# Rotary embedding: unit 0's second half loaded by one SyncE transfer with 16 KB rows and stored from GpSimd

## The chip, the cores and the metric

One core of a Trainium2 chip. The metric is the device time of one execution in microseconds (us). In the profile PE is TensorE, DVE VectorE, ACT ScalarE, POOL GpSimd, SP SyncE. L72 is line 72 of the kernel, and the lines of the changed kernel and of the experiments are shifted by a few. A ratio below is the mean time of one kernel's fast runs over that of the other's of the same rounds, so not quite the ratio of the medians quoted beside it. Each experiment was timed beside the kernel before on the same chip.

## The reference

```
angles = outer(positions * scale, freqs)          # 1024 x 32
cos, sin = cos(angles), sin(angles)
out_first  = x_first * cos - x_second * sin       # x: 8 x 8 x 1024 x 64, float32
out_second = x_first * sin + x_second * cos
```

16.8 MB are read and 16.8 MB written; the arithmetic is small. The sin/cos table is made on the core, from two tiny inputs: positions (8 KB) and frequencies (128 bytes).

## The kernel before

x is cut into four units of 4 MB, each spread over 128 partitions with 8192 values a row. GpSimd's loads cast float32 to float16 on the way. Only the second half of unit 0 is loaded as float32 (X0f) and cast by ScalarE, which brings it in without GpSimd.

```
X0f = xout.tile([P, N], FP32, tag="O")
Q = NH // 2                                                         # NH = 4096 values, 16 KB
nc.sync.dma_start(out=X0f[:, :Q], in_=xv[0][:, NH : NH + Q])        # 1 MB, 8 KB rows
nc.scalar.dma_start(out=pos_i64, in_=positions...)                  # 128 rows of 64 B
nc.scalar.dma_start(out=freq_row, in_=freqs[None, :])               # 1 row of 128 B
nc.scalar.dma_start(out=X0f[:, Q:NH], in_=xv[0][:, NH + Q :])       # 1 MB, 8 KB rows
...
nc.gpsimd.dma_start(out=Xf[0][:, :NH], in_=xv[0][:, :NH])           # unit 0, first half, cast
for u in range(1, NU): nc.gpsimd.dma_start(out=Xf[u], in_=xv[u])    # units 1 to 3, cast
... # table: matmul of freq_row, VectorE, two sines, 16 matmuls that spread it, copies to T
nc.scalar.copy(out=Xf[0][:, NH:], in_=X0f[:, :NH])                  # behind the copies to T
for u in range(NU):
    for s in range(2):                                              # halves
        ... # VectorE: two products, one subtraction, one addition
        nc.scalar.copy(out=OUT[:, ns], in_=Xf[u][:, ns])
        if u in (0, NU - 1):
            nc.sync.dma_start(out=ov[u][:, ns], in_=OUT[:, ns])     # 2 MB
    if u not in (0, NU - 1):
        nc.gpsimd.dma_start(out=ov[u], in_=OUT)                     # 4 MB
```

The order on each engine is pinned to the order of the program.

## Time and profile before

84.41 us, median of 6 runs (84.1 to 84.78); the profiled execution has a span of 82.5 us.

| what | us |
|---|---|
| positions land / frequencies land | 5.74 / 5.45 |
| the table's first step on VectorE (y) starts | 6.22 |
| first product of the main loop starts | 13.07 |
| unit 2's store is issued | 59.37 |
| VectorE's last instruction ends | 69.5 |

To read it, look for what can be late without cost. VectorE is busy without a gap in the main loop, but it ends 13 us before the span does; the DMA engines are at work almost from end to end. The lines are in the prediction.

### The profile page before, as it was taken

What the parts mean: (1) busy time and instruction counts of PE and PEld (TensorE: products, weight loads), DVE (VectorE), ACT (ScalarE), POOL (GpSimd) and SP (SyncE); (2) the same over time, 40 slices, a digit from 0 to 9 for tenths busy, and PEclk for the clock granted to TensorE, in tenths of its full rate; (3) what the DMA queues carried; (4) which work ended last, traced back from release to release, by engine and by line L of the source; (5) the groups of instructions that cost most, each with busy time, mean ns of one, the idle gap of its engine ahead of it and who ended that gap; (6) DMA issues with size and microseconds to landing.
All of it is one profiled execution on the core that took longest, in us unless ns stands there. A gap on an engine that the chain in (4) does not pass through costs nothing.

```text
span 82.5 us, 179 instructions
## 1 busy us (share of the span) xinstructions
PE 7.1 (9%) x18; PEld 2.8 (3%) x18; DVE 60.3 (73%) x40; ACT 40.1 (49%) x18; POOL 4.6 (6%) x14
## 2 busy tenths in 40 slices
PE   0020999200000000000000000000000000000000
PEld 0020333000000000000000000000000000000000
DVE  0306476999999999999999999999999997000000
ACT  0603069999950790393098059219606902940000
POOL 4920000000000000000000200000200000000000
PEclk9999999985555555555555555555555555555555
DMA  2899998997996999799979999996998999799990
GB/s 48 336 319 278 290 326 187 254 246 159 230 254 127 254 262 342 270 278 350 278 191 302 270 342 421 461 524 286 508 509 350 413 508 461 302 445 429 397 485 24
DMA packets 1874, 26.22 MB, mean 318 GB/s; under 512 B 338, under 2 KB 338, under 8 KB 338
## 3 DMA queue, kind: packets, MB, share of 16 engines
q0 software_dynamic: 864, 15.73, 66.2%
q1 hardware_dynamic: 720, 9.44, 27.5%
q10 hardware_dynamic: 290, 1.06, 3.3%
HBM read 16.79 MB, written 16.78 MB: 407 GB/s over the span
## 4 chain that ended last, share of the span: by engine, by line
DVE 55%; ACT 15%; issue 6%; DMA 5%; PE 5%; DVEq 1%; ACTq 0%
DVE X L153 20%; DVE pr L152 20%; DVE X L157 9%; DVE X L154 6%; DMA freq_row<-in_freqs_dram 5%; ACT T L139 5%; ACT OUT L160 4%; PE ps L129 4%; ACT X L140 4%; DVEq L193 1%; PE cfreq L97 1%; ACT tab L122 1%; DVE r L113 1%; DVE y L104 1%; ACTq L69 0%
## 5 line engine op out<-in xcount | busy, mean ns | idle before, releaser
L160 ACT CAST OUT<-X 128x4096 f32<-128x4096 f16 x8 | 28.9, 3607 | 24.2 <-DVE X L157 24.2
L152 DVE TENSOR_TENSOR pr<-X,T 128x4096 f16<-128x4096 f16 x8 | 18.3, 2292 | 1.0 <-ACT T L139 0.7
L153 DVE TENSOR_TENSOR X<-X,T 128x4096 f16<-128x4096 f16 x8 | 18.3, 2292 | 0.3
L154 DVE TENSOR_TENSOR X<-X,pr 128x2048 f16<-128x2048 f16 x8 | 9.8, 1225 | 0.3
L157 DVE TENSOR_TENSOR X<-pr,X 128x2048 f16<-128x2048 f16 x8 | 9.7, 1218 | 0.0
L139 ACT CAST T<-ps 128x1024 f16<-128x1024 f32 x6 | 5.7, 1028 | 2.6 <-PE ps L129 2.6
L129 PE MATMUL ps<-tab,sel 128*128 128x512 f16 x16 | 6.5, 599 | 2.2 <-ACT tab L122 2.2
L164 POOL DMA_DIRECT2D out_dram<-OUT x2 | 1.1, 538 | 54.1 <-ACT OUT L160 54.1
L137 DVE CAST T<-ps 128x1024 f16<-128x1024 f32 x2 | 2.5, 1225 | 2.2 <-PE ps L129 2.2
L140 ACT CAST X<-X0f 128x4096 f16<-128x4096 f32 x1 | 3.6, 3649 | 0.0
L95 DVE COPY sel<-one 128x2048 f16<-128x2048 f16 x1 | 0.7, 693 | 2.8 <-POOL one L87 2.8
L129 PEld LDWEIGHTS <-sel 128*128 128x128 f16 x16 | 2.3, 143 | 6.1 <-issue 6.1
L117 ACT ACTIVATE tab<-r 128x256 f16<-128x256 f32 x1 | 0.4, 418 | 4.1 <-DVE r L113 4.1
L117 ACT ACT_TABLE_LOAD x1 | 1.3, 1283 | 2.1 <-issue 2.1
L92 POOL DMA_DIRECT2D X<-in_x_dram x3 | 2.0, 658 | 0.0
L100 DVE CAST posf<-pos_i 128x8 f32<-128x8 int32 x1 | 0.2, 172 | 2.3 <-DMA pos_i<-in_positions_dram 2.3
L97 PE MATMUL cfreq<-freq_row,coef 1*128 1x32 f32 x2 | 0.6, 392 | 5.6 <-DMA freq_row<-in_freqs_dram 5.6
L83 POOL DMA_DIRECT2D X<-in_x_dram x1 | 0.7, 669 | 0.8 <-POOLq L179 0.8
L97 PEld LDWEIGHTS cfreq<-freq_row,coef 1*128 1x128 f32 x2 | 0.5, 306 | 5.6 <-issue 5.6
L104 DVE TENSOR_TENSOR y<-posf,cfreq 128x256 f32<-128x256 f32 x1 | 0.4, 422 | 0.3 <-PE cfreq L97 0.3
L122 ACT ACTIVATE tab<-ra,quarter 128x256 f16<-128x256 f32 x1 | 0.5, 507 | 0.0
L113 DVE SCALAR_TENSOR_TENSOR r<-m,y 128x256 f32<-128x256 f32 x1 | 0.4, 424 | 0.0
(10 smaller groups left out, 1.9 us busy)
## 6 DMA issues: line engine op xcount, KB each, us to landing
out_dram<-OUT SPq DMA_DIRECT2D x4, 2048.0 KB, 14.8
out_dram<-OUT POOLq DMA_DIRECT2D x2, 4096.0 KB, 15.3
X<-in_x_dram POOLq DMA_DIRECT2D x3, 2048.0 KB, 31.9
X0f<-in_x_dram SPq DMA_DIRECT2D x1, 1024.0 KB, 4.8
X<-in_x_dram POOLq DMA_DIRECT2D x1, 1024.0 KB, 11.7
X0f<-in_x_dram ACTq DMA_DIRECT2D x1, 1024.0 KB, 13.2
pos_i<-in_positions_dram ACTq DMA_DIRECT2D x1, 8.0 KB, 5.0
freq_row<-in_freqs_dram ACTq DMA_DIRECT2D x1, 0.1 KB
```

Of the source, the lines that this page charges most:

```text
L92: pin(nc.gpsimd.dma_start(out=Xf[u], in_=xv[u]))
L97: nc.tensor.matmul(out=cfreq, lhsT=coef, rhs=freq_row, start=True, stop=True)
L117: pin(nc.scalar.activation(out=tab[:, 0], in_=r, func=AF.Sin, bias=0.0, scale=-_TWO_PI_DN))
L129: nc.tensor.matmul(out=ps[:, i].rearrange("p t w -> p (t w)"), lhsT=sel[:, g + i].rearrange("s h q -> s (h q)"), rhs=tab.rearrange("s t k ...
L137: pin(nc.vector.tensor_copy(out=dst, in_=ps))
L139: pin(nc.scalar.copy(out=dst, in_=ps))
L140: pin(nc.scalar.copy(out=Xf[0][:, NH:], in_=X0f[:, :NH]))
L152: pin(nc.vector.tensor_tensor(out=pr, in0=Xs, in1=sin_b, op=ALU.mult))
L153: pin(nc.vector.tensor_tensor(out=Xs, in0=Xs, in1=cos_b, op=ALU.mult))
L154: pin(nc.vector.tensor_tensor(out=Xs[:, :, 0, :], in0=Xs[:, :, 0, :], in1=pr[:, :, 1, :], op=ALU.subtract))
L157: pin(nc.vector.tensor_tensor(out=Xs[:, :, 1, :], in0=pr[:, :, 0, :], in1=Xs[:, :, 1, :], op=ALU.add))
L160: pin(nc.scalar.copy(out=OUT[:, ns], in_=Xf[u][:, ns]))
```

## The change

The intent: one transfer with larger rows instead of two for X0f, ScalarE's queue free for the small inputs, and the store of unit 0's second half behind GpSimd's loads, so that it takes no DMA time from them.

```
-    Q = NH // 2
-    pin(nc.sync.dma_start(out=X0f[:, :Q], in_=xv[0][:, NH : NH + Q]))
+    pin(nc.sync.dma_start(out=X0f[:, :NH], in_=xv[0][:, NH:]))
...
-    pin(nc.scalar.dma_start(out=X0f[:, Q:NH], in_=xv[0][:, NH + Q :]))
...
             if u in (0, NU - 1):
-                pin(nc.sync.dma_start(out=ov[u][:, ns], in_=OUT[:, ns]))
+                eng = nc.gpsimd if (u, s) == (0, 1) else nc.sync
+                pin(eng.dma_start(out=ov[u][:, ns], in_=OUT[:, ns]))
```

## The prediction

> **What bounds the kernel now.** I read the page first: the share of each engine, the row of DMA over 40 slices, the three DMA queues. VectorE is busy 73% of the span; the 16 DMA engines are busy nearly always.
>
> ```profile
> DVE  0306476999999999999999999999999997000000
> ACT  0603069999950790393098059219606902940000
> DMA  2899998997996999799979999996998999799990
> ...
> q0 software_dynamic: 864, 15.73, 66.2%
> q1 hardware_dynamic: 720, 9.44, 27.5%
> q10 hardware_dynamic: 290, 1.06, 3.3%
> HBM read 16.79 MB, written 16.78 MB: 407 GB/s over the span
> ```
>
> The reader is to see two candidates for the bound: VectorE without a gap from slice 7 to 33, and DMA at 8 or 9 almost from end to end (q0 is GpSimd's queue, q1 SyncE's, q10 ScalarE's; the three add up to 97% of 16 engines' span). Packets are counted where they start, so single slices wobble; the table by stretches of 10 us settles it (the last two figures of a row are the DMA share and GB/s):
>
> ```profile
> 2.00:12.00 10.00, 4.18 (x11) 1.91 (x12) 4.35 (x8) 3.20 (x4) 2.60 (x7) 1.00 1.00 301
> ...
> 42.00:52.00 10.00, 0.00 (x0) 0.00 (x0) 9.86 (x6) 6.56 (x2) 0.54 (x1) 0.50 1.08 356
> 52.00:62.00 10.00, 0.00 (x0) 0.00 (x0) 9.86 (x7) 3.63 (x2) 0.53 (x1) 0.50 1.00 429
> 62.00:72.00 10.00, 0.00 (x0) 0.00 (x0) 7.42 (x5) 6.05 (x2) 0.00 (x0) 0.50 0.96 416
> 72.00:81.00 9.00, 0.00 (x0) 0.00 (x0) 0.00 (x0) 1.17 (x1) 0.00 (x0) 0.50 0.96 411
> ```
>
> From 2 to 81 us the DMA engines have no idle stretch. So the kernel is bound by DMA: 79 us of packets, a start of about 1.8 us before the first byte and about 1.3 us after the last. A reordering of the same bytes can't shorten 79 us; it can only open a hole. The question is then whether the DMA engines are ever left without work, and that is set by when stores become ready, that is by the chain of computation. The chain of waits over the first 17 us (start, duration, what):
>
> ```profile
> 1.16 4.29 DMA freq_row<-in_freqs_dram
> 5.45 0.14 issue
> 5.58 0.61 PE cfreq L97 x2
> 6.20 0.02 issue
> 6.22 0.43 DVE y L104
> ...
> 8.42 3.59 PE ps L129 x8
> ```
>
> and of VectorE's list of waits:
>
> ```profile
> DVE posf L100 <- DMA pos_i<-in_positions_dram: 2.3, 1, 2.3
> ...
> DVE pr L152 <- ACT T L139: 0.7, 1, 0.7
> ```
>
> So the main loop starts when the sin/cos table T is spread, at 13.07 us, and the table starts when two tiny transfers on ScalarE's queue land: frequencies at 5.45, positions at 0.74 + 5.0 = 5.74. From 13.07 on VectorE runs to 69.5 without waiting for anything. A delay of the tiny transfers goes one to one into every store.
>
> **What the Trainium skill says.** "DMA: Bandwidth & Descriptors", section "Queues, rings and completion order": each DMA engine goes round-robin over the queue rows that have work, a packet a turn. The trace agrees, and tells the size of a turn. This is the DMA view of the 0.64 us from 3.50 (packets, MB, share of 16 engines):
>
> ```profile
> q1 hardware_dynamic: 34, 0.28, 102.6%
> q10 hardware_dynamic: 33, 0.00, 3.5%
> ```
>
> 34 rows of 8 KB against 33 rows of 64 B: one for one. Turns go by rows, not by bytes. A row of 8 KB takes 1.026 x 16 x 0.64 / 34 = 0.309 us, a 64 B row about 0.011 us. The same page, section "Issuing engines are not separate DMA queues": spreading transfers over issuers saves only issue time. The table above agrees: the share is about 1.0 whichever queues are at work. Section "Latency and other measured facts": first byte about 1 us for GpSimd's transfers; no run here isolates it yet, and SyncE's first packet comes about 1.0 us after its issue at 0.74.
>
> **The change part by part.**
>
> 1. *The load.* X0f is 2 MB either way. Before: 1 MB in 8 KB rows from SyncE, 1 MB in 8 KB rows from ScalarE behind positions and frequencies. After: 2 MB in 16 KB rows from SyncE, issued first. Positions are 128 rows of 64 B, 8 to a DMA engine, and each takes its turn behind one SyncE row. The cost of a 16 KB row, from the last 20 us, where SyncE's stores have such rows: the DMA view of 61.4 to 81.2 has 49.5% for that queue, so 0.495 x 16 x 19.8 / 256 = 0.61 us. Positions are therefore done 8 x (0.61 - 0.31) = 2.4 us later at least, and the frequencies, one packet behind them in the same queue, too.
>
> 2. *GpSimd's load cutting in.* Here are the 0.3 us from 4.70 before:
>
> ```profile
> q0 software_dynamic: 10, 0.08, 130.0%
> q1 hardware_dynamic: 14, 0.03, 27.6%
> q10 hardware_dynamic: 27, 0.00, 5.8%
> ```
>
> GpSimd's first rows start here, just as SyncE's MB ends; before 4.70 no GpSimd packet is seen. After the change SyncE has some 5 of its 8 rows per engine begun at 4.7 (first at 1.76, the second about 1 us later, then 0.62 apart). If GpSimd's rows enter the rotation at the same moment as before, three more turns have a GpSimd row in them, at 0.62 us each (66.3% of 16 engines over 6 us, 102 rows: 0.663 x 96 / 102). That is another 1.9 us. Whether they enter is not told by this trace: packets already taken up may go first. So the delay D of positions and frequencies is 2.4 us (no cutting in) to 4.3 us (all of it). I take 3.3.
>
> 3. *From D to the loop.* y, table, matmuls and T copies have the same durations, so T is there at 13.07 + D. The other inputs are not in the way: GpSimd's first half lands at 1.25 + 11.7 = 12.95, and its bytes plus X0f's are the same sum. The X0f cast on ScalarE starts at 16.55, behind T copies, and moves with T. So every store is ready D later.
>
> 4. *The store of unit 0, second half.* Moved from SyncE's queue (issued 30.97, landing 26.4 us later because it alternates with the loads) to GpSimd's, behind the loads. Loads then end earlier by the 4.9 us or less that this half took from them, but VectorE waits for no load, so that earns nothing. Unit 3 needs that buffer at about 62.6 + D; behind the loads the half would be done at about 52. No cost, no gain. The issue costs GpSimd some 0.53 us, and it is idle.
>
> 5. *From late stores to the end.* The loads, unit 0 and unit 1 keep the DMA engines busy to about 61.4 before (the DMA view of 49.3 to 61.4 has exactly 128 data packets and 16 completions of GpSimd's queue: unit 1). Their sum does not change, so the queue runs dry there. What follows is unit 2:
>
> ```profile
> 59.37 0.53 POOL L164 DMA_DIRECT2D out_dram<-OUT  x1 [13.55 <-ACT OUT L160]
> ```
>
> Issued at 59.37, 0.53 us of issue and about 1 us to the first byte (the skill's figure, an estimate): ready at 60.9, so 0.5 us of slack. With D = 3.3 it is ready at 64.2, a hole of 2.8 us in DMA work. Behind it are 4 MB of unit 2 and 2 + 2 MB of unit 3, 19.5 us of packets, which stay contiguous: unit 3's halves are ready at 67.2 + D and 74.2 + D, before unit 2's and the first half's packets end. The earlier place, before unit 1's store (ready 46.8 + D against dry at about 51.7), does not open below D = 4.9.
>
> Sum: + D - 0.5 = 3.3 - 0.5 = 2.8 us, less 0.1 for a few packets fewer: + 2.7.
>
> **The rivals.**
>
> *Nothing moves (the transfers are hidden anyway).* The bytes are the same and DMA is the bound. For it: the slack at 61.4, which could be larger than I think if GpSimd's first byte is quicker, up to 1.5 us; then D = 2.4 gives only +0.9, some 85.4. Against it: the chain shows that the frequencies' landing is on the path with no slack at all.
>
> *ScalarE's queue with only small inputs lets them land sooner: faster.* For it: ScalarE's big half is gone and 2 to 4% could be won if DMA's bound were not there. Against it: that half is behind the small inputs in its queue and never delays them (they land by 5.74, its rows begin after 5.3). And even a table 1 us earlier finds the DMA engines full. About 84.3.
>
> *GpSimd's store as a new trouble.* The skill, same page, "SWDGE vs HWDGE vs iDMA": GpSimd writes descriptors to SBUF and VectorE can lock it out. The two stores that GpSimd issues amid VectorE's work take 0.54 us, against 0.67 for its first load, so I see no lock here; were it there, another 1 to 2 us before unit 0's half, which nothing waits for.
>
> *Full cutting in*: D = 4.3, +3.8, 88.3.
>
> **Range and chances.** D of 2.4 gives +1.9 (86.4), D of 4.3 gives +3.8 (88.3), the middle 87.2. I say 87.1 us. The range 85.7 to 88.6 adds 0.7 below for more slack and 0.3 above. The line for slower is 84.51 x 1.02 = 86.2: it takes D - slack above 1.7, which fails only where no cutting in and a larger slack meet. Slower 0.77, within 2% 0.21, faster 0.02.
>
> **What would show it.** The frequencies' piece in the chain, 4.29 us before, should be 6.7 to 8.6; the first product of the main loop at 15.5 to 17.4 instead of 13.07; ScalarE's queue with 16 KB rows of SyncE one for one; VectorE's 56.4 us of loop unchanged; a dent in DMA near 61 to 64. The loads' landing (46.0 us for the last) should be some microseconds earlier, to no avail. I am wrong if positions land near 5.7, if the main loop starts late but the end does not move (slack larger), or if the hole opens elsewhere.

## The result, and the profile after

The changed kernel takes 89.02 us (median of 6 runs, 88.31 to 89.17): ratio 1.0527, 95% interval 1.048 to 1.0574. It is slower, as predicted, but by 4.6 us and not by 2.7, and the time is outside the range. The profiled span went from 82.5 to 87.2 us.

The chain of waits of the changed kernel in its first microseconds (start, duration, what):

```profile
1.16 10.24 DMA freq_row<-in_freqs_dram
11.40 0.14 issue
11.54 0.62 PE cfreq L95 x2
12.15 0.02 issue
12.18 0.43 DVE y L102
```

The frequencies' piece has grown from 4.29 to 10.24 us, and y starts at 12.18 instead of 6.22. VectorE's list of waits says the same of the positions (2.3 us before), and that the main loop still waits for the table alone:

```profile
DVE posf L98 <- DMA pos_i<-in_positions_dram: 7.2, 1, 7.2
...
DVE pr L151 <- ACT T L137: 0.4, 1, 0.4
```

The main loop starts at 18.79, 5.72 us later than before (the table's way from y to the loop happened to be 0.24 us quicker). The loop is as long as before. Where this reaches the end is seen in the table by stretches of the changed kernel (the last two columns are the share of the DMA engines and GB/s):

```profile
52.00:62.00 10.00, 0.00 (x0) 0.00 (x0) 9.86 (x7) 4.42 (x2) 0.00 (x0) 0.50 0.98 419
62.00:66.00 4.00, 0.00 (x0) 0.00 (x0) 3.93 (x3) 2.79 (x1) 0.53 (x1) 0.50 0.00 0
66.00:76.00 10.00, 0.00 (x0) 0.00 (x0) 9.14 (x6) 4.33 (x2) 0.00 (x0) 0.50 1.01 431
```

For 4 us the DMA engines have nothing to do: everything up to unit 1 is stored, and unit 2's store is only issued at 65.09, as its line of the timeline shows:

```profile
65.09 0.53 POOL L164 DMA_DIRECT2D out_dram<-OUT  x1 [13.56 <-ACT OUT L159]
```

This is the hole that the prediction described, at the place where it said. Its size is what was off. It is also not alone: before unit 1's store, issued at 50.99, the DMA engines run dry for a moment too, the earlier place that the prediction held closed below D = 4.9. The same table from 51.5 to 52 us has packets for 0.02 of the DMA engines' time:

```profile
51.50:52.00 0.50, 0.00 (x0) 0.00 (x0) 0.47 (x2) 0.00 (x0) 0.02 (x1) 0.50 0.02 0
```

By the packets of the trace, a DMA engine stands idle for 0.42 us there on average (16 last completions end at 51.73 in the mean, 16 first rows start at 52.15) and for 4.33 us at the large hole; together they are the growth of the span. The sum can be checked over the kernels that have the hole: from the issue of unit 2's store to the end of the span are 87.2 - 65.09 = 22.1 us here, and 22.1 in three of the experiments below (load_only 87.4 - 65.31, freq_first 88.5 - 66.44, freq_none 86.2 - 64.07); the fourth, rows_4k, has 88.6 - 66.05 = 22.5 (its last packet ends 1.7 us before the span does, 1.2 in the changed kernel; why is not known). Before, it was 82.5 - 59.37 = 23.1: there the store waited some 1.0 us for the DMA engines. So 5.72 us of delay less 1.0 us of slack make the 4.7 us by which the span grew.

### The profile page after: what moved, and what is told of

Its sections match the earlier page's. It is cut to its first block, busy times and chain, and to the rows that moved or that the text cites. A ratio compares the mean times of both kernels' runs of the same rounds, so it can differ in the third digit from the quotient of the medians.

```text
span 87.2 us, 177 instructions
## 1 busy us (share of the span) xinstructions
PE 6.0 (7%) x18; PEld 2.4 (3%) x18; DVE 60.3 (69%) x40; ACT 40.1 (46%) x18; POOL 5.1 (6%) x15
## 4 chain that ended last, share of the span: by engine, by line
DVE 52%; ACT 14%; DMA 12%; issue 5%; PE 5%; DVEq 1%; ACTq 0%
DVE X L152 18%; DVE pr L151 18%; DMA freq_row<-in_freqs_dram 12%; DVE X L156 8%; DVE X L153 6%; ACT T L137 5%; ACT OUT L159 4%; ACT X L138 4%; PE ps L127 4%; DVEq L193 1%; PE cfreq L95 1%; ACT tab L120 1%; DVE r L111 1%; DVE y L102 0%; ACTq L68 0%
## 5 line engine op out<-in xcount | busy, mean ns | idle before, releaser
L127 PE MATMUL ps<-tab,sel 128*128 128x512 f16 x16 | 5.4, 485 | 2.8 <-ACT tab L120 2.2
L164 POOL DMA_DIRECT2D out_dram<-OUT x2 | 1.1, 531 | 27.1 <-ACT OUT L159 27.1
L162 POOL DMA_DIRECT2D out_dram<-OUT x1 | 0.5, 543 | 32.3 <-ACT OUT L159 32.3
## 6 DMA issues: line engine op xcount, KB each, us to landing
out_dram<-OUT POOLq DMA_DIRECT2D x2, 4096.0 KB, 11.7
X<-in_x_dram POOLq DMA_DIRECT2D x1, 1024.0 KB, 11.7
```

The costliest lines, as they stand in the source:

```text
L127: nc.tensor.matmul(out=ps[:, i].rearrange("p t w -> p (t w)"), lhsT=sel[:, g + i].rearrange("s h q -> s (h q)"), rhs=tab.rearrange("s t k ...
```

## The experiments

My theory after the result: all of the loss is in the load. On every DMA engine the queues take turns by rows, whatever their size, so that 16 KB rows, and GpSimd's rows among them, hold up the 64 B rows of positions and all that is behind them in ScalarE's queue. The rivals: the store from GpSimd makes the hole; the megabytes ahead count and not the rows; the changed kernel's DMA work is itself longer.

**load_only and store_only: one half of the change each.** load_only has the store back on SyncE; store_only is the kernel before with the one store moved:

```
-                pin(nc.sync.dma_start(out=ov[u][:, ns], in_=OUT[:, ns]))
+                eng = nc.gpsimd if (u, s) == (0, 1) else nc.sync
+                pin(eng.dma_start(out=ov[u][:, ns], in_=OUT[:, ns]))
```

> The changed load with the old store (unit 0's second half back on SyncE). Theory (turns): the loss is all in the load, since 16 KB rows delay positions and frequencies; frequencies land at about 11.4 us, the main loop starts at about 18.8, time 89.0 (88.3 to 89.7). Rival (store): the store behind GpSimd's loads makes the hole in DMA work; then this run is near 84.4, or between.

> The old load with the changed store (unit 0's second half from GpSimd). Theory: no cost, no gain, 84.4 (84.0 to 84.9), although the loads land some us earlier. Rival (store): 86 or more.

load_only: 89.14 us, ratio 1.0572 (1.0552 to 1.0593). store_only: 84.33 us, ratio 1.0001 (0.9978 to 1.0024). The load is all of the loss. With the store moved, the last load of x did land earlier, 43.5 us after its issue instead of 46.0, and nothing waited for it. The rival of the store falls.

**before_light and after_light: what bounds the two kernels.** In each, the subtraction and the addition on VectorE are left out (a wrong result), 19.5 us of VectorE's 60:

```
-            pin(nc.vector.tensor_tensor(
-                out=Xs[:, :, 0, :], in0=Xs[:, :, 0, :], in1=pr[:, :, 1, :], op=ALU.subtract))
-            pin(nc.vector.tensor_tensor(
-                out=Xs[:, :, 1, :], in0=pr[:, :, 0, :], in1=Xs[:, :, 1, :], op=ALU.add))
```

> The kernel before without the subtraction and the addition on VectorE (wrong result on purpose): 19.5 us of VectorE's 60 us are gone. Theory (DMA bounds the kernel before): 83.6 to 84.6, within 1% of 84.4, as the same packets fill the DMA engines. Rival (VectorE's chain bounds it): 70 to 78.

> The changed kernel without the subtraction and the addition (wrong result on purpose). Theory: the small inputs still land near 11, but unit 2's store is ready long before 61 us, the hole in DMA work closes, and the time is that of the kernel before: 83.8 to 84.8. Rival (the changed kernel loses in its DMA work itself, by rows or queues): 88 to 89.

before_light: 84.47 us, ratio 1.0016 (0.9989 to 1.0042). A third of VectorE's work is worth nothing: the kernel before is bound by DMA. VectorE now waits for loads instead, as its list of waits in before_light shows:

```profile
DVE pr L152 <- DMA X<-in_x_dram: 7.6, 3, 5.5
```

after_light: 84.09 us, ratio 0.997 (0.9955 to 0.9986). Positions still land 9.9 us after their issue there, but stores are ready early enough, and the stretch that was empty is full:

```profile
62.00:66.00 4.00, 0.00 (x0) 0.00 (x0) 0.00 (x0) 0.00 (x0) 0.00 (x0) 0.50 1.00 430
```

So the changed kernel's DMA work is not longer; if anything it is 0.3% shorter. What it loses it loses by the hole.

**rows_8k and rows_4k: the size of SyncE's rows.** The changed kernel with its 2 MB in two transfers of 8 KB rows, and in four of 4 KB rows, all on SyncE:

```
-    pin(nc.sync.dma_start(out=X0f[:, :NH], in_=xv[0][:, NH:]))
+    for q in range(2):            # rows_4k: range(4), and NH // 4
+        qs = slice(q * NH // 2, (q + 1) * NH // 2)
+        pin(nc.sync.dma_start(out=X0f[:, qs], in_=xv[0][:, NH + q * NH // 2 : NH + (q + 1) * NH // 2]))
```

> The changed kernel, but SyncE loads the same 2 MB by two DMAs with 8 KB rows. Theory (turns go by rows): the 8 rows of positions per engine are through at about 5 us as before; then the completion, the frequencies and their completion each wait for a turn of 0.31 + 0.62, so frequencies land at about 8.2, the loop starts at about 15.9, and with 0.95 us of slack the time is about 86.3 (85.6 to 87.0). Rival (bytes: what counts is the 2 MB ahead on SyncE's queue): frequencies at 11.4 and 89.0.

> The changed kernel, but SyncE loads the same 2 MB by four DMAs with 4 KB rows. Theory (turns go by rows): positions' 8 turns cost about 0.165 us each, so positions and frequencies land by about 5.0, earlier than in the kernel before; then GpSimd's first half, landing near 12.95, starts the loop, and DMA bounds the time: 84.4 (84.0 to 85.0). Rival (bytes): 89.0; if fewer, larger rows are worth something in themselves: above 85.

rows_8k: 84.36 us, ratio 1.0006 (0.9985 to 1.0027). The same 2 MB on the same queue as in the changed kernel, in rows of half the size, and the whole loss is gone: rows count, not bytes ahead. (It is two transfers instead of one as well; that this alone does nothing was not tested.) Yet my number was 2 us too high. I had GpSimd's rows come in at 4.7 us; the DMA view of rows_8k from 2.4 to 5.2 us shows one of them (q0) in all that time, while ScalarE's queue (q10) is through:

```profile
q1 hardware_dynamic: 145, 1.07, 91.8%
q10 hardware_dynamic: 142, 0.01, 3.4%
q0 software_dynamic: 1, 0.01, 1.4%
```

The frequencies' row starts at 5.08, just ahead of GpSimd's first at 5.17, and the frequencies count as landed at 5.79. It is a race, and half-size rows win it.

rows_4k: 90.28 us, ratio 1.0717 (1.0691 to 1.0743): a miss of 6 us. The small inputs did land early (positions 4.1 us after issue), but now X0f itself is the small-rowed one. In the DMA view from 5.4 to 10.8 us SyncE (q1) and GpSimd (q0) take turns again, 4 KB against rows that are 16 KB in memory (counted here as the 8 KB that are written):

```profile
q0 software_dynamic: 112, 0.92, 80.9%
q1 hardware_dynamic: 113, 0.46, 22.3%
```

X0f's last quarter landed at 23.18 us, the cast waited for it, and VectorE for the cast:

```profile
DVE pr L153 <- ACT X L140: 7.7, 1, 7.7
```

My expectation had followed the rule for one transfer and forgotten it for the other.

**load_held and freq_none: the terms of the delay.** load_held keeps GpSimd's load back until positions have landed; freq_none has a constant for the frequencies (a wrong result):

```
# load_held
+    pin(nc.gpsimd.tensor_copy(out=held, in_=pos_i64...))    # waits for positions
     pin(nc.gpsimd.dma_start(out=Xf[0][:, :NH], in_=xv[0][:, :NH]))
# freq_none
-    pin(nc.scalar.dma_start(out=freq_row, in_=freqs[None, :]))
+    pin(nc.gpsimd.memset(freq_row, 0.01))
```

> The changed kernel, but GpSimd issues its load of unit 0's first half only when positions have landed (a small copy waits for them), so that no GpSimd row can cut in. To be read from the profile, not from the time. Theory (terms of the delay): 16 KB rows of SyncE alone cost 8 x 0.30 = 2.4 us, so frequencies land at 7.6 to 8.0 instead of 11.40, and positions at 7.7 to 8.2. Rival (the large rows alone make the whole delay): 10.5 to 11.4. The time should be near 87, since GpSimd's load is now late and leaves the DMA engines empty for a while.

> The changed kernel without the load of the frequencies, a constant in their place (wrong result on purpose). Theory: the frequencies, behind positions in their queue, cost two turns more behind GpSimd's rows, so that without them positions (landing at 10.6, as in the changed kernel) set the table, which starts at 10.95 instead of 12.18: 1.2 us less, 87.8 (87.4 to 88.2). Rival (the frequencies cost nothing beyond positions): 89.0.

load_held ran once, 87.2 us, with a profile and of unknown state; only its early timeline is used. freq_none: 87.95 us, ratio 1.0433 (1.0408 to 1.0457), as expected. The start of y in load_held, then in freq_none:

```profile
8.99 0.42 DVE L104 TENSOR_TENSOR y<-posf,cfreq 128x256 f32<-128x256 f32 x1 [0.55 <-PE cfreq L97]
```

```profile
10.98 0.42 DVE L102 TENSOR_TENSOR y<-posf,cfreq 128x256 f32<-128x256 f32 x1
```

The landing of positions is to be read beside these starts, as y can wait for the frequencies instead (in load_held it does, for 0.55 us). Positions were issued at 0.74 in each kernel and landed 5.0 us later before, 9.9 in the changed kernel, and in load_held:

```profile
DMA to landing us min/median/max: 7.5/7.5/7.5
```

These are the terms:

- 16 KB rows alone: 7.5 - 5.0 = 2.5 us.
- GpSimd's rows cutting in on positions: 9.9 - 7.5 = 2.4. Of this, 1.86 are three turns of the rows (the last row of positions starts at 9.57 instead of 7.71), and the rest is a further turn: the completions of positions, the 16 packets of 4 B that follow the rows in the trace, also wait behind a GpSimd row.
- The frequencies behind them in the same queue: 12.18 - 10.98 = 1.20, by y's start.

Together they are 6.1 us. The delay of y is 12.18 - 6.22 = 5.96, as y waited for the frequencies by some 0.15 us before the change already.

The turns themselves are seen in the DMA view of the changed kernel from 5.5 to 9.2 us, one row of each queue in turn:

```profile
q0 software_dynamic: 48, 0.39, 50.6%
q1 hardware_dynamic: 48, 0.79, 50.6%
q10 hardware_dynamic: 50, 0.00, 0.9%
```

and from 9.2 to 11.1 us, where SyncE's queue has only its 16 completions left, and the last 14 rows of positions, their 16 completions, the frequencies' row and its completion (32 in all) have turns behind GpSimd's rows:

```profile
q0 software_dynamic: 50, 0.41, 102.7%
q10 hardware_dynamic: 32, 0.00, 1.8%
q1 hardware_dynamic: 16, 0.00, 1.2%
```

**freq_first, small_ahead and sync_late: the order in which the queues start.** freq_first swaps the two transfers on ScalarE; small_ahead has positions on SyncE ahead of X0f; sync_late has the frequencies there, so that X0f is issued at 1.14 instead of 0.74, after positions on ScalarE:

```
# freq_first:   scalar: freqs, positions       sync: X0f
# small_ahead:  scalar: freqs                  sync: positions, X0f
# sync_late:    scalar: positions              sync: freqs, X0f
```

> The changed kernel with the order on ScalarE's queue swapped: frequencies, then positions. Theory: in the changed kernel the frequencies are last in their queue and pay turns for the completion of positions, for themselves and for their own completion; swapped they land before 5 us, and positions at about 11.0 set the table, which starts at 11.25 instead of 12.18: time 88.1 (87.7 to 88.6). Rival (all is over once the rows of positions are through; the frequencies add nothing): 89.0.

> The changed kernel with positions on SyncE ahead of its 16 KB rows and frequencies alone on ScalarE. Theory: both land near 3 us, the table is ready near 10.5, the loop starts near 13.0 when GpSimd's half lands, and the time is bound by DMA: 84.4 to 84.9 (SyncE's load is issued 0.4 us later). A gain over the kernel before would mean that its table start costs it something: below 83.8. If the large rows hurt otherwise than by delaying the two small inputs, 86 or more.

> The changed kernel with the frequencies on SyncE ahead of its 2 MB, so that this is issued 0.4 us after positions instead of with them. Theory (a DMA engine takes up some 80 KB of a queue ahead, and a queue that comes later waits behind it): positions' rows are taken up first, SyncE's large rows come behind them, both small inputs land near 3 us, the time is 84.4 to 84.9. Rival (strict turns from the first moment): positions still alternate with 16 KB rows, land at 9.5 to 10.7, and the time is 87.5 to 88.2.

freq_first: 90.25 us, ratio 1.0686 (1.0656 to 1.0717): a miss in direction. Positions, issued at 1.28 instead of 0.74, landed at 12.99 instead of 10.6. The DMA view from 2.3 to 5.5 us has one line of queues, SyncE's; no row of positions moved for 3.2 us:

```profile
q1 hardware_dynamic: 65, 1.06, 80.0%
```

That is no turn-taking at all. It looks as if a DMA engine takes up rows of a queue ahead of time and a later queue waits behind them: 80 of X0f's rows, 5 to a DMA engine or 80 KB, start before the first row of positions at 5.52. GpSimd's first row comes in behind 80 of them in the changed kernel too, at 5.56, 4.3 us after its issue, while with empty DMA engines (load_held) it took 1.4 us. sync_late was made to test that, with the roles exchanged. Its 144 packets of positions (128 rows, 16 completions) are all through between 1.7 and 2.1 us, and no large row is seen:

```profile
q10 hardware_dynamic: 144, 0.01, 21.0%
```

sync_late: 84.68 us, ratio 1.004 (1.0015 to 1.0065). An order of 0.4 us at the start decides some 8 us of positions' landing (1.7 us after issue here, 9.9 in the changed kernel). But the run does not separate the two theories, as it was meant to: X0f's first row starts at 2.12, when the last packet of positions has begun at 2.07, so strict turns had nothing to alternate with. Against strict turns speaks freq_first alone. That rows are taken up ahead fits all of these runs; it is not shown, and how many, and where they are held, I did not measure separately.

small_ahead: 84.52 us, ratio 1.0026 (1.0011 to 1.0042). So 16 KB rows do no harm in themselves, once the small inputs are out of the way. Nor does an earlier table help: there VectorE's loop starts at 13.52, when GpSimd's half lands, and DMA bounds the time. Both versions are 0.3 to 0.4% above the kernel before, probably because X0f is issued 0.4 us later; that was not tested alone. No run beats the kernel before with a right result: its DMA engines are never idle between their start and their end.

## Why the prediction was right or wrong

- *DMA is the bound, and the change can only open a hole*: right (before_light, after_light, and the empty stretch from 62 to 66 us). It missed that the earlier place opens too: D went above its 4.9, and 0.42 us are lost there.
- *The store costs and earns nothing*: right (store_only).
- *Rows take turns one for one, 16 KB rows cost 2.4 us*: right, 2.5 us measured.
- *GpSimd's rows cut in, between none and 1.9 us*: all of it for the rows of positions, 1.86 us. I could not tell from the trace and took about half. That it was three turns is luck in part: at 4.7 us SyncE had begun 4 rows on each DMA engine and not 5, but GpSimd's rows came in only at 5.56, after 5.
- *"The frequencies, one packet behind them in the same queue, too"*: this is the step that failed. The prediction gave the frequencies the same delay as positions and counted 8 turns. But completions and the frequencies' row need turns of their own. Before, these turns cost next to nothing, as ScalarE's queue was through just when GpSimd's rows began; after, they are taken behind rows of 0.62 us: some 0.54 us for the completions of positions and 1.20 for the frequencies and theirs, of which 0.15 were there before. These 1.6 us put D at 5.96 for y and 5.72 for the loop, above the stated maximum of 4.3.
- *0.5 us of slack*: measured 1.0, as GpSimd's first byte came 1.1 us after the start of the issue of unit 2's store, and not 1.5. The prediction had added the 0.53 us of the issue to the 1 us; the measured 1.1 us contain it.

In the sum, D - slack: predicted 3.3 - 0.5 = 2.8, measured 5.72 - 1.0 = 4.7. The term D was mis-sized by 2.4 us: 1.6 are the turns not counted, 1.0 the share of cutting in (1.86 against 0.9) and 0.1 the rows, less the 0.24 by which the table was quicker.

## What to carry to other kernels

In a kernel bound by DMA a change of transfers is judged by whether the DMA engines ever run dry, so find the store that is issued with the least slack and follow back what it waits for. Where a tiny transfer with many rows stands at the head of that chain, look at what starts beside it: in these runs SyncE's large rows, and GpSimd's behind them, delayed it by 4.9 us, and issuing it first (small_ahead, sync_late) or halving the rows beside it (rows_8k) removed the loss. Coalescing into larger rows was not free for the neighbours, and splitting was not free for the transfer that was split (rows_4k), as here a queue's share was set by the size of its rows against the others'.

## What the Trainium skill lacked or had wrong

- "DMA: Bandwidth & Descriptors", section "Queues, rings and completion order": turns at packet granularity are right, but the packet of typically 9 to 17 descriptors isn't what these runs show. One row was one turn, of 64 B as of 16 KB (34 rows of 8 KB against 33 of 64 B in 0.64 us; 48, 48 and 50 rows of three queues in 3.7 us). It also lacks that completions take turns (in the changed kernel those of positions start at 9.86 to 10.19 on 14 of the 16 DMA engines, one GpSimd row of 0.62 us after their last row).
- The same section lacks what freq_first shows: positions, issued 0.5 us after X0f, got no row for 3.2 us, until 80 rows of X0f (5 to a DMA engine) had started. Issued 0.4 us ahead of X0f instead (sync_late), all 144 packets were through in 0.4 us.
- The same page, section "Issuing engines are not separate DMA queues": that the choice of issuer only saves issue time holds for the total (DMA share about 1.0 wherever there is work), but not for when a transfer lands. The same 8 KB landed 1.7, 5.0, 9.9 or 11.7 us after issue depending on the queue, the order and the neighbour's rows, and the kernel took between 84.4 and 90.3 us.
- The same page, section "Latency and other measured facts": about 1 us to the first byte of a GpSimd transfer agrees from the start of the issue (unit 2's store issued at 65.09 into idle DMA engines, data from 66.18). The 0.6 us for SyncE agrees only from its end: in the changed kernel the issue runs from 0.74 to 1.12 and no packet is seen before 1.72, so 0.6 us from the end and 1.0 from the start. The page does not say from where the two are counted.
